# Reordering side work in a two-block transformer kernel: activation sums behind loads, filler between attention stages, sums ahead of taps

## The chip, the cores and the metric

The kernel runs on one core of one Trainium2 chip. The metric is the device time of one execution in microseconds (us). Engines are TensorE (PE, with its weight loads PEld), VectorE (DVE), ScalarE (ACT), GpSimd (POOL) and SyncE (SP, which here issues DMAs).

## The reference

Two transformer blocks run one after the other on a sequence of 1024 tokens of width 1024, all in fp32. The first is a hybrid layer; the second an attention block with a convolutional FFN:

```python
def hybrid_layer(x, ...):
    h = rms_norm(x, norm_g)
    u = jnp.einsum('bsd,dc->bsc', h, w_in)
    v_c, b_c, c_c, z_c, q, k, v, z_a, gate_logits = jnp.split(u, SPLIT_POINTS, axis=-1)
    y_c = b_c * causal_depthwise_conv(c_c * v_c, conv_w) * jax.nn.silu(z_c)
    y_a = jnp.einsum('bsc,cd->bsd', y_c, w_conv_out)
    o = sliding_window_attention(q, k, v, sinks) * jax.nn.silu(z_a)   # q, k normed per head
    y_b = jnp.einsum('bsc,cd->bsd', o, w_attn_out)
    g_a, g_b = jnp.split(jax.nn.sigmoid(gate_logits + gate_b), 2, axis=-1)
    return x + jnp.einsum('bsd,de->bse', g_a * y_a + g_b * y_b, w_out)

def conv_ffn(x, w_up, conv_w, conv_b, w_down):        # FFN_DIM 2816
    u, g = jnp.split(x @ w_up, [FFN_DIM], axis=-1)
    g = causal_dwconv(g, conv_w, conv_b)
    return (jax.nn.gelu(g, approximate=False) * u) @ w_down

def second_block(x, p, ...):
    x = layer_norm(x * ALPHA + fox_mixer(x, ...))     # causal attention with forget gates
    x = layer_norm(x * ALPHA + conv_ffn(x, ...))
    return x + sigmoid(x @ ple_w_gate + ple_b_gate) * (p @ ple_w_proj)
```

The sliding attention has 16 query heads on 4 key heads, blocks of 128 queries and a window of 128.

## The kernel before, in words

Every fp32 product is three matmuls of rounded operands: high by high, high by low, low by high. An operand is split into its halves by a rounding copy on ScalarE (`hi`, L84: names ending in `h`) and a subtraction on VectorE (`lo`, L88 and L90: names ending in `l`). A weight tile is loaded by SyncE into `wraw` (L157) and split into `wh` and `wl`. `gemm_ws` (L173, matmuls L181 to L183) takes eight k tiles, 24 matmuls 128x512, with the weights stationary; `gemm_xs` (L186, L196 and L197) does it with the activations stationary. PSUM has eight banks, each for one 128x512 result.

**Pairs.** Large products are done by a scheme of seven products in place of eight (`seven`, L437). Sums of operand quarters (`X7.build`, L380 for the additions; results `xsh` and `xsl`) are made once; per pair of column tiles the weights' sums are made (`Pairs`, L481 to L553), their halves are `pwh`, `pwl` and `pwo`. A product is 12 matmuls (L433 to L435), in the program's order 1, 2, 6, 5, 7, 3, 4. At product 6 the next pair's weights are loaded, at 7 its first quarter is split (`first`), at 3 its second part is made (`second`), at 4 its third (`third`). Products 1 and 2 read `x2Th` and `x2Tl` in the FFN, the others mostly the sums.

**Attention of the first block** (`attn1_stream`, L631). For 32 items (four groups of heads by eight token tiles) a software pipeline runs stages: `a1` projects, `a2` norms and transposes, `a3` makes scores and exponentials (L696, L704), `a3b` the sums' reciprocal on VectorE (L718) and the normalisation of `p` on GpSimd (L720), `a4` transposes `p` (L731), `a5` multiplies by the values (L745, L746). The loop at L764 calls one stage of five items in turn. `weave` (L32) mixes this stream with the convolution branch and the gates by the cost that each stream yields: the attention goes on while its cost stays under `RATIO` times the other's.

**The FFN.** The last step of the second attention (`attn_out`, L1341) adds, norms (POOL L1370) and stores `x2` per token tile (L1371), and `to_T` (L933) transposes it (L938) into `x2Th` and `x2Tl`. The transposes of the last three tiles are kept in `attn_out.last` and are done in `up_plain` (L1430), which makes the first three column tiles of the inner activation by `gemm_ws`, as `pg0`, `pu0`, `pg1` in the first of them; `ffn_conv` makes the taps (L1404 to L1409) and the gelu. Beside these tiles (L1455 to L1472) the seven products' sums `x7.build` run, a piece at every other step. Then 19 pairs make the other column tiles (L1515). `keep` (L1415) stores the inner activation of two column tiles: three quarters as they are and four sums of quarters (`hs`), made on VectorE, as the operands of the down product: seven stores into `h_d` on SyncE (L1420 to L1429).

The order of each engine's instructions is set by a scheduler, which runs the program on a timeline of its own and hands out tiles from pools (46 of 128x1024 in `t4`, 8 in `y2`).

Of the kernel before, what the change touches and what calls it, by code (L numbers as in the profile page):

```python
# [11 lines left out]
HP = 400  # L12
LAG = 3
NP = 6
RATIO = 1.9
NCONV, NG, NTR = 3, 1, 5
N4, N2 = 46, 8
NPLAIN = 3
# [38 lines left out]
def tile_two_blocks(ctx: ExitStack, tc: tile.TileContext, I, out, dbg=None):  # L57
# [130 lines left out]
    def gemm_xs(x, t, wk, n, ps=None, step=2, kts=range(KT)):  # L188

        if ps is None:  # L190
            ps = bank()
        c = max(107.0, n / 2.4)
        for kt in kts:
            xh, xl = x.sta(kt, t)
            wh, wl = wk(kt)
            pe.matmul(ps[:, :n], lhsT=xh, rhs=wh, start=kt == kts[0], stop=False)  # L196
            pe.matmul(ps[:, :n], lhsT=xh, rhs=wl, start=False, stop=False)  # L197
            pe.matmul(ps[:, :n], lhsT=xl, rhs=wh, start=False, stop=kt == kts[-1])
            if kt % step == step - 1:
                yield 3 * step * c  # L200
        return ps
# [430 lines left out]
    def attn1_stream():  # L632
# [3 lines left out]
        def a1(n):  # L636
            g, t = divmod(n, 8)
            if t == 0:
                grp[g] = dict(W=[wqa.get(0) for _ in range(4)])
                grp[g]["V"] = t4((128, 8, 128), F32R, "V")  # L640
            G = grp[g]
            ps = yield from gemm_xs(hT, t, lambda kt: tuple(p[:, kt % 2, :] for p in G["W"][kt // 2]), 384)
            V = G["V"]
            raw = t2((128, 384), name="qkv")
            act.activation(raw, ps[:, :384], AF.Copy)
            hi(V[:, t, 0:64], ps[:, 320:384])
            sq = t2((128, 320), name="sq")
            dve.tensor_tensor(out=sq, in0=raw[:, :320], in1=raw[:, :320], op=OP.mult)
            ss = sm(5)
            dve.tensor_reduce(out=ss, in_=sq.rearrange("p (h d) -> p h d", d=64), axis=mybir.AxisListType.X,  # L650
                              op=OP.add)
            lo(V[:, t, 64:128], raw[:, 320:384], V[:, t, 0:64])
            r = rstd_of(ss, 5, 1.0 / 64, 1e-6)
            qn = t2((128, 384), name="qn")
            dve.tensor_tensor(out=qn[:, :320].rearrange("p (h d) -> p h d", d=64),
                              in0=raw[:, :320].rearrange("p (h d) -> p h d", d=64),
                              in1=r[:, :, None].to_broadcast([128, 5, 64]), op=OP.mult)
            dve.tensor_scalar(qn[:, 320:384], raw[:, 256:320], r[:, 4:5], None, op0=OP.mult)
            st[n] = dict(qn=qn)
# [104 lines left out]
        for n in range(N + 4):  # L764
            if n < N:
                yield from a1(n)
            if 0 <= n - 2 < N:
                yield from a3(n - 2)
            if 0 <= n - 1 < N:
                yield from a2(n - 1)  # L770
            if 0 <= n - 2 < N:
                a3b(n - 2)
            if 0 <= n - 3 < N:
                yield from a4(n - 3)
            if 0 <= n - 4 < N:
                yield from a5(n - 4)
# [654 lines left out]
    def up_plain(ct, first=False):  # L1431
        wg = wq.get()
        if first:

            pg0 = yield from gemm_ws(wg, x2T, 0)
            wu = wq.get()
            attn_out.last.popleft()()
            attn_out.last.popleft()()
            pu0 = yield from gemm_ws(wu, x2T, 0)
            attn_out.last.popleft()()  # L1440
            pg1 = yield from gemm_ws(wg, x2T, 1)
        gs = t4(name="gs")
        for hf in range(2):
            ps = (pg0, pg1)[hf] if first else (yield from gemm_ws(wg, x2T, hf))
            act.activation(gs[:, HS[hf]], ps, AF.Copy)
        y = ffn_conv(ct, gs)
        if not first:
            wu = wq.get()
        for hf in range(2):
            ps = pu0 if first and hf == 0 else (yield from gemm_ws(wu, x2T, hf))  # L1450
            tt(dve, y[:, HS[hf]], ps, y[:, HS[hf]], OP.mult)
        keep(ct, y)
# [3 lines left out]
    for ct in range(NPLAIN):  # L1456
        for _ in up_plain(ct, first=ct == 0):
            n += 1
            if n == 13:
                build = chain(x7.build(0), x7.build(1))  # L1460
            if n % 2:
                next(build, None)
            if n == 26:
                upairs.load(0)
            elif n == 34:
                upairs.first(0)
            elif n == 40:
                upairs.second(0)
            elif n == 44:
                upairs.third(0)  # L1470
# [28 lines left out]
    def split_down():  # L1499
# [5 lines left out]
            ops2.append((h, l))  # L1505
        raw_down()

    def end_up(i):
        if i == 2:
            for _ in range(4):  # L1510
                raw_down()
        elif i in (3, 4):
            split_down()

    for ct in range(NPLAIN, NCT):  # L1515
        gs, u = upairs.run(end_up if ct == NCT - 1 else None)
        y = ffn_conv(ct, gs)
        tt(dve, y, y, u, OP.mult)
        keep(ct, y)
    split_down()  # L1520

    def residual(t):
# [145 lines left out]
```

## Time and profile before

| what | us |
| --- | --- |
| median of three runs | 2528.01 (2527.15 to 2532.12) |
| profiled execution, its own time | 2526.26 |
| its span | 2524.6 |
| TensorE busy | 2448.2 |
| VectorE busy | 1610.2 |
| ScalarE busy | 1070.2 |
| GpSimd busy | 449.6 |

All times of the trace are counted from the span's start. The mean granted TensorE clock is 0.989 of full speed. The first attention ends at about 424 us, the FFN begins at about 1732, its pairs run from about 1797 to 2215.

### The profile page before, as it was taken

How to read it: one execution, taken by the hardware profiler on the slowest of the kernel's cores; microseconds unless marked ns; L12 is line 12 of the kernel's file. 1: busy time of each engine (PE TensorE's matmuls, PEld its weight loads, DVE VectorE, ACT ScalarE, POOL GpSimd, SP SyncE). 2: the span in 40 equal slices, each digit the busy share in tenths (PEclk: the TensorE clock that was granted, in tenths of full speed). 3: DMA queues.
4: the chain of work that ended last, by engine and by line, in shares of the span. 5: the costliest groups of instructions: out<-in, count | busy, mean ns of one | idle time of the engine just before them, and what ended most of it. 6: DMA issues, size and time to landing. Idle time of an engine off the chain costs nothing. (4 is left out here: it accounts for less than half of the span.)

```text
span 2524.6 us, 33221 instructions
## 1 busy us (share of the span) xinstructions
PE 2448.2 (97%) x12330; PEld 2083.1 (83%) x12330; DVE 1610.2 (64%) x2936; ACT 1070.2 (42%) x1978; POOL 449.6 (18%) x498
## 2 busy tenths in 40 slices
PE   8999998999999999999999999999899999999999
PEld 7988987888888788888989898887677777788887
DVE  4777777666765436325575656567877777676873
ACT  4656566323333312126565656542423232354321
POOL 2322232000000045012323323413000000000331
PEclk9999998999999999999999999999999999999999
DMA  5021111322253889321111122332223232396512
GB/s 166 22 61 53 37 42 51 100 75 67 59 175 109 292 313 369 134 76 52 59 51 59 43 66 85 134 109 92 67 82 102 81 112 81 125 359 229 186 68 84
DMA packets 242924, 285.77 MB, mean 113 GB/s; under 512 B 21826, under 2 KB 166730, under 8 KB 242762
## 3 DMA queue, kind: packets, MB, share of 16 engines
q1 hardware_dynamic: 242762, 283.65, 34.4%
q8 instruction: 97, 1.59, 0.3%
q14 instruction: 65, 0.53, 0.1%
HBM read 206.72 MB, written 76.87 MB: 112 GB/s over the span
## 5 line engine op out<-in xcount | busy, mean ns | idle before, releaser
L433 PE MATMUL ps<-xsh,pwh 128*128 128x512 f32 x456 | 179.2, 393 | 8.0 <-ACT pwh L84 8.0
L434 PE MATMUL ps<-xsl,pwh 128*128 128x512 f32 x456 | 178.4, 391 | 0.0
L88 DVE TENSOR_TENSOR pwl<-wraw,pwh 128x1024 fp32r<-128x1024 f32 x114 | 138.5, 1221 | 60.4 <-ACT pwh L84 60.3
L435 PE MATMUL ps<-xsh,pwl 128*128 128x512 f32 x456 | 171.4, 390 | 0.0
L84 ACT ACTIVATE pwh<-wraw 128x1024 fp32r<-128x1024 f32 x114 | 118.1, 1051 | 112.8 <-DVE wraw L380 104.0
L84 ACT ACTIVATE wh<-wraw 128x1024 fp32r<-128x1024 f32 (+3 forms) x105 | 105.5, 1016 | 73.6 <-DMA wraw<-in_ple_w_gate_dram 18.8
L1337 POOL TENSOR_SCALAR sm<-sm 128x1 f32<-128x1 f32 x16 | 11.6, 724 | 698.0 <-DVE sm L1335 698.0
L1535 PE MATMUL ps<-dh,dl 128*128 128x512 f32 x308 | 119.8, 389 | 0.0
L1534 PE MATMUL ps<-dl,dh 128*128 128x512 f32 x308 | 119.8, 389 | 0.0
L88 DVE TENSOR_TENSOR wl<-wraw,wh 128x1024 fp32r<-128x1024 f32 (+1 forms) x77 | 92.1, 1205 | 43.2 <-ACT wh L84 36.5
L1533 PE MATMUL ps<-dh 128*128 128x512 f32 x308 | 118.1, 390 | 0.0
L88 DVE TENSOR_TENSOR phl<-ps,phl 128x512 fp32r<-128x512 f32 (+1 forms) x160 | 97.3, 633 | 31.9 <-ACT phl L84 30.6
L181 PE MATMUL ps<-hTh,wh 128*128 128x512 f32 x288 | 115.2, 400 | 2.3 <-DVE hTl L90 2.2
L433 PE MATMUL ps<-x2Th,pwh 128*128 128x512 f32 x228 | 93.2, 409 | 22.3 <-ACT pwh L84 22.3
L182 PE MATMUL ps<-hTl,wh 128*128 128x512 f32 x288 | 114.3, 397 | 0.0
L183 PE MATMUL ps<-hTh,wl 128*128 128x512 f32 x288 | 114.3, 397 | 0.0
L84 ACT ACTIVATE dh<-dr 128x1024 fp32r<-128x1024 f32 x77 | 80.2, 1059 | 71.1 <-PE ps L1535 33.4
L433 PEld LDWEIGHTS ps<-xsh,pwh 128*128 128x128 f32 x456 | 86.2, 189 | 28.1 <-ACT pwh L84 10.4
L88 DVE TENSOR_TENSOR dl<-dr,dh 128x1024 fp32r<-128x1024 f32 x77 | 91.9, 1220 | 25.5 <-ACT dh L84 13.9
L380 DVE TENSOR_TENSOR wraw<-wraw 128x512 f32<-128x512 f32 x152 | 105.0, 691 | 4.3
L380 POOL TENSOR_TENSOR wda<-wda 128x512 f32<-128x512 f32 x11 | 15.1, 1377 | 516.7 <-DMA wda<-in_ffn_w_down_dram 495.2
L181 PE MATMUL ps<-x1Th,wh 128*128 128x512 f32 x256 | 101.7, 397 | 1.4 <-DVE QB L90 1.4
(341 smaller groups left out, 7496.1 us busy)
## 6 DMA issues: line engine op xcount, KB each, us to landing
wraw<-in_w_in_dram SPq DMA_DIRECT2D x56, 512.0 KB, 4.4
wraw<-in_ffn_w_up_dram SPq DMA_DIRECT2D x44, 512.0 KB, 6.6
dr<-h_d SPq DMA_DIRECT2D x77, 256.0 KB, 3.5
wraw<-in_attn_w_in_dram SPq DMA_DIRECT2D x22, 512.0 KB, 4.3
h_d<-hs SPq DMA_DIRECT2D x44, 256.0 KB, 2.8
dr<-t_d SPq DMA_DIRECT2D x44, 256.0 KB, 4.3
h_d<-yc SPq DMA_DIRECT2D x33, 256.0 KB, 2.3
dr<-in_ffn_w_down_dram SPq DMA_DIRECT2D x33, 256.0 KB, 5.4
```

The lines of the kernel that those rows point to most:

```text
L84: act.activation(dst, src, AF.Copy, scale=1.0 if scale is None else scale)
L88: (eng or dve).tensor_tensor(out=dst, in0=src, in1=f(h), op=OP.subtract)
L181: pe.matmul(ps, lhsT=w[0][:, kt, :], rhs=xh, start=kt == 0, stop=False)
L182: pe.matmul(ps, lhsT=w[0][:, kt, :], rhs=xl, start=False, stop=False)
L183: pe.matmul(ps, lhsT=w[1][:, kt, :], rhs=xh, start=False, stop=kt == KT - 1)
L380: e.tensor_tensor(out=out, in0=a, in1=b, op=op)
L433: pe.matmul(ps, lhsT=w[0][:, c], rhs=xh, start=st, stop=False, skip_group_check=more)
L434: pe.matmul(ps, lhsT=w[0][:, c], rhs=xl, start=False, stop=False, skip_group_check=more)
L435: pe.matmul(ps, lhsT=w[1][:, c], rhs=xh, start=False, stop=q == 3, skip_group_check=more)
L1533: pe.matmul(ps[j], lhsT=h[:, 0, c], rhs=h[:, 1, :], start=m == 0, stop=False)
L1534: pe.matmul(ps[j], lhsT=h[:, 0, c], rhs=l[:, 1, :], start=False, stop=False)
L1535: pe.matmul(ps[j], lhsT=l[:, 0, c], rhs=h[:, 1, :], start=False, stop=m == NM - 1)
```

## The change

Six edits. (1) `RATIO` goes from 1.9 to 2.1. (2) In `a1`, the next group's first weights are loaded at token tile 6 and split at tile 7, in place of when the group begins. (3) In the four last rounds of the attention's loop, which have no `a1`, the stream yields a cost of 7000 (the other stream's turns are counted in the same unit, ns), so that `weave` gives the other branch a turn there. (4) In the first column tile of the FFN all three kept transposes go behind `pu0`; two of them were ahead. (5) The seven products' sums begin at step 9 in place of 13 and run at every step up to 12, then at every odd one. (6) `keep` of a column tile is done at product 5 of the next pair (behind the load of the pair after, at product 6), in place of right behind its own.

```diff
@@ -12,7 +12,7 @@
 HP = 400
 LAG = 3
 NP = 6
-RATIO = 1.9
+RATIO = 2.1
 NCONV, NG, NTR = 3, 1, 5
 N4, N2 = 46, 8
 NPLAIN = 3
@@ -639,6 +639,10 @@
                 grp[g] = dict(W=[wqa.get(0) for _ in range(4)])
                 grp[g]["V"] = t4((128, 8, 128), F32R, "V")
             G = grp[g]
+            if t == 6:
+                wqa.fetch(2)
+            elif t == 7 and wqa.raw:
+                wqa.split()
             ps = yield from gemm_xs(hT, t, lambda kt: tuple(p[:, kt % 2, :] for p in G["W"][kt // 2]), 384)
             V = G["V"]
             raw = t2((128, 384), name="qkv")
@@ -764,6 +768,8 @@
         for n in range(N + 4):
             if n < N:
                 yield from a1(n)
+            else:
+                yield 7000.0
             if 0 <= n - 2 < N:
                 yield from a3(n - 2)
             if 0 <= n - 1 < N:
@@ -1434,10 +1440,9 @@
 
             pg0 = yield from gemm_ws(wg, x2T, 0)
             wu = wq.get()
-            attn_out.last.popleft()()
-            attn_out.last.popleft()()
             pu0 = yield from gemm_ws(wu, x2T, 0)
-            attn_out.last.popleft()()
+            for _ in range(3):
+                attn_out.last.popleft()()
             pg1 = yield from gemm_ws(wg, x2T, 1)
         gs = t4(name="gs")
         for hf in range(2):
@@ -1456,9 +1461,9 @@
     for ct in range(NPLAIN):
         for _ in up_plain(ct, first=ct == 0):
             n += 1
-            if n == 13:
+            if n == 9:
                 build = chain(x7.build(0), x7.build(1))
-            if n % 2:
+            if n < 13 or n % 2:
                 next(build, None)
             if n == 26:
                 upairs.load(0)
@@ -1505,7 +1510,14 @@
             ops2.append((h, l))
         raw_down()
 
+    kept = deque()
+
+    def beside_up(i):
+        if i == 5 and kept:
+            keep(*kept.popleft())
+
     def end_up(i):
+        beside_up(i)
         if i == 2:
             for _ in range(4):
                 raw_down()
@@ -1513,10 +1525,11 @@
             split_down()
 
     for ct in range(NPLAIN, NCT):
-        gs, u = upairs.run(end_up if ct == NCT - 1 else None)
+        gs, u = upairs.run(end_up if ct == NCT - 1 else beside_up)
         y = ffn_conv(ct, gs)
         tt(dve, y, y, u, OP.mult)
-        keep(ct, y)
+        kept.append((ct, y))
+    keep(*kept.popleft())
     split_down()
 
     def residual(t):
```

Lines of the changed kernel are up to ten higher than those of the kernel before at the same place. Three excerpts of the order follow, each of before and then of the change.

SyncE between an odd column tile's pair and the next pair. `wraw` are a pair's two weight loads, `h0` to `h6` the stores of the inner activation, `yc` its column tiles, `hs` its sums. Before:

```order
L1422 DMA h3_d_284<-yc_17738 128x512
L1429 DMA h4_d_285<-hs_17747 128x512
L1429 DMA h5_d_286<-hs_17748 128x512
L1429 DMA h6_d_287<-hs_17749 128x512
L157 DMA wraw_17794<-in_ffn_w_up_2_dram 128x8x128
L1429 DMA h2_d_283<-hs_17750 128x512
L157 DMA wraw_17796<-in_ffn_w_up_2_dram 128x8x128
L157 DMA wraw_17924<-in_ffn_w_up_2_dram 128x8x128
```

and now:

```order
L157 DMA wraw_17651<-in_ffn_w_up_2_dram 128x8x128
L1426 DMA h0_d_281<-yc_17608 128x512
L157 DMA wraw_17779<-in_ffn_w_up_2_dram 128x8x128
L157 DMA wraw_17781<-in_ffn_w_up_2_dram 128x8x128
L1427 DMA h1_d_282<-yc_17738 128x512
L1428 DMA h3_d_284<-yc_17738 128x512
L1435 DMA h4_d_285<-hs_17800 128x512
L1435 DMA h5_d_286<-hs_17801 128x512
L1435 DMA h6_d_287<-hs_17802 128x512
```

The loads of the next pair stand ahead of all of its stores but `h0`, and the six others ahead of the pair after.

TensorE at the end of the first attention: the last scores (L697, L701), the transposes of `p` (L731, L735), the product with the values (L745 and L746, L749 and L750) and gate projection (L181 to L183). `p1_4637` before and `p1_4589` now are the last item but one, `p1_4686` now the last. Before:

```order
L697 MATMUL ps_4717<-KL_3792,Q_4665 128x256
L697 MATMUL ps_4726<-KL_3792,Q_4665 128x256
L696 MATMUL ps_4726<-KH_3791,Q_4665 128x256
L697 MATMUL ps_4726<-KL_3792,Q_4665 128x256
L731 MATMUL ps_4745<-ident_71,p1_4637 128x128
L731 MATMUL ps_4754<-ident_71,p1_4637 128x128
L745 MATMUL ps_4763<-ph_4684,V_3589 128x512
L746 MATMUL ps_4763<-pl_4685,V_3589 128x512
L745 MATMUL ps_4763<-ph_4693,V_3589 128x512
```

and now, from the last but one's value product to the last item's transposes:

```order
L750 MATMUL ps_4735<-pl_4643,V_3541 128x512
L749 MATMUL ps_4735<-ph_4651,V_3541 128x512
L750 MATMUL ps_4735<-pl_4652,V_3541 128x512
L182 MATMUL ps_4667<-hTl_419,wh_4150 128x512
L183 MATMUL ps_4667<-hTh_418,wl_4151 128x512
L181 MATMUL ps_4760<-hTh_184,wh_4563 128x512
...
L181 MATMUL ps_4760<-hTh_232,wh_4563 128x512
L182 MATMUL ps_4760<-hTl_233,wh_4563 128x512
L183 MATMUL ps_4760<-hTh_232,wl_4564 128x512
L735 MATMUL ps_4773<-ident_71,p1_4686 128x128
L735 MATMUL ps_4782<-ident_71,p1_4686 128x128
```

Before, the transposes come directly behind scores; now 26 projection matmuls (20 of them in the gap) stand ahead of those of the last item.

ScalarE at the start of the FFN: the evictions of the transposes (`x2Th`, L84) and the split of the next weights (`wh_16856`). Before, the end of the second kept set, the weights, and the third:

```order
L84 ACTIVATE x2Th_16806<-ps_16892 128x2x128
L84 ACTIVATE x2Th_16813<-ps_16897 128x2x128
L84 ACTIVATE wh_16856<-wraw_16827 128x1024
L1445 ACTIVATE gs_16972<-ps_16831 128x512
L84 ACTIVATE x2Th_16792<-ps_16927 128x2x128
```

and now:

```order
L84 ACTIVATE x2Th_16806<-ps_16803 128x2x128
L84 ACTIVATE x2Th_16813<-ps_16810 128x2x128
L84 ACTIVATE wh_16856<-wraw_16827 128x1024
L84 ACTIVATE x2Th_16792<-ps_16887 128x2x128
L84 ACTIVATE x2Th_16799<-ps_16892 128x2x128
L84 ACTIVATE x2Th_16806<-ps_16897 128x2x128
```

The weights' split stands ahead of all three kept sets' evictions, where it stood ahead of one.

## Rows read from the trace of the kernel before

**Rows 1.** The page's first part: busy us of each engine, share of the span, x instructions.

```profile
PE 2448.2 (97%) x12330; PEld 2083.1 (83%) x12330; DVE 1610.2 (64%) x2936; ACT 1070.2 (42%) x1978; POOL 449.6 (18%) x498
```

**Rows 2.** The list of TensorE's waits over the span: line of the waiting matmul, releaser, us in total, times, longest us.

```profile
PE ps L433 <- ACT pwh L84: 30.3, 10, 8.0
PE ps L731 <- POOL p L720: 8.4, 7, 3.6
...
PE ps L938 <- POOL xn L1370: 2.4, 1, 2.4
```

**Rows 3.** The page's grouped lines, the one of the products that read x2Th: busy us, mean ns of one, idle us before them and what ended most of it.

```profile
L433 PE MATMUL ps<-x2Th,pwh 128*128 128x512 f32 x228 | 93.2, 409 | 22.3 <-ACT pwh L84 22.3
```

**Rows 4.** Windows of 100 us, a full stretch first: length, busy us and (x instructions) of PE, PEld, DVE, ACT and POOL, the granted clock, DMA share, GB/s.

```profile
500.00:600.00 100.00, 100.00 (x440) 82.16 (x439) 66.36 (x80) 33.34 (x40) 0.00 (x0) 1.00 0.23 69
1800.00:1900.00 100.00, 87.69 (x364) 70.47 (x363) 69.60 (x83) 32.22 (x38) 0.00 (x0) 0.93 0.29 85
1900.00:2000.00 100.00, 94.35 (x397) 77.07 (x396) 71.89 (x85) 34.09 (x40) 0.00 (x0) 0.95 0.29 87
2000.00:2100.00 100.00, 95.45 (x418) 77.72 (x417) 73.44 (x89) 32.15 (x37) 0.00 (x0) 1.00 0.27 82
2100.00:2200.00 100.00, 91.47 (x391) 73.66 (x390) 69.27 (x85) 32.04 (x38) 0.00 (x0) 0.98 0.40 124
```

**Rows 5.** Windows of 10 us behind long waits of TensorE, the same columns.

```profile
410.00:420.00 10.00, 6.29 (x20) 4.17 (x18) 9.96 (x17) 7.04 (x16) 4.69 (x6) 0.67 0.00 0
420.00:430.00 10.00, 8.13 (x27) 6.05 (x28) 4.91 (x7) 2.79 (x5) 2.03 (x2) 0.67 0.00 0
1740.00:1750.00 10.00, 7.45 (x28) 5.84 (x29) 6.45 (x14) 2.87 (x6) 4.30 (x4) 0.83 0.83 237
1820.00:1830.00 10.00, 9.33 (x30) 7.29 (x31) 4.19 (x4) 3.74 (x5) 0.00 (x0) 0.69 0.38 105
1850.00:1860.00 10.00, 7.82 (x28) 5.68 (x27) 5.68 (x9) 2.28 (x3) 0.00 (x0) 0.84 1.02 283
1940.00:1950.00 10.00, 9.86 (x32) 7.91 (x33) 7.55 (x9) 4.55 (x7) 0.00 (x0) 0.72 0.43 109
1980.00:1990.00 10.00, 7.83 (x28) 6.04 (x27) 6.67 (x9) 3.96 (x6) 0.00 (x0) 0.83 0.80 220
2110.00:2120.00 10.00, 10.00 (x39) 8.12 (x40) 8.43 (x11) 5.07 (x6) 0.00 (x0) 0.86 0.17 43
```

**Rows 6.** The timeline of SyncE's DMA issues between two pairs; columns: start in us from the span's start, us, engine, line, operation, out<-in, shape, count, and in brackets the idle time before it and what ended it.

```profile
1848.15 1.33 SPq L1429 DMA_DIRECT2D h_d<-hs  x3
1849.57 0.44 SPq L157 DMA_DIRECT2D wraw<-in_ffn_w_up_dram  x1
...
1851.04 4.06 SPq L157 DMA_DIRECT2D wraw<-in_ffn_w_up_dram  x3
```

**Rows 7.** The timeline of VectorE at the same place, same columns.

```profile
1845.66 1.23 DVE L380 TENSOR_TENSOR yc<-yc,pb 128x1024 f32<-128x1024 f32 x1 [1.19 <-ACT yc L1409]
1846.92 0.69 DVE L380 TENSOR_TENSOR hs<-yc 128x512 f32<-128x512 f32 x1
```

**Rows 8.** The timeline of ScalarE at the same place, same columns.

```profile
1854.47 1.06 ACT L84 ACTIVATE pwh<-wraw 128x1024 fp32r<-128x1024 f32 x1 [0.38 <-DMA wraw<-in_ffn_w_up_dram]
```

**Rows 9.** The timeline of TensorE at the same place: the last matmul of one pair and the first of the next.

```profile
1853.07 0.39 PE L435 MATMUL ps<-xsh,pwl 128*128 128x512 f32 x1
1855.58 0.50 PE L433 MATMUL ps<-x2Th,pwh 128*128 128x512 f32 x1 [2.12 <-ACT pwh L84]
```

**Rows 10.** The timeline of TensorE at the end of the first attention, the transposes (L731) behind a wait.

```profile
409.62 0.69 PE L731 MATMUL ps<-ident,p 128*128 128x128 f32 x2 [2.37 <-POOL p L720]
...
416.78 0.69 PE L731 MATMUL ps<-ident,p 128*128 128x128 f32 x2 [3.57 <-POOL p L720]
```

**Rows 11.** The timeline of ScalarE there: table load, gate, the last item's exponentials (one of four shown).

```profile
407.81 1.28 ACT L794 ACT_TABLE_LOAD   x1
409.10 0.69 ACT L794 ACTIVATE gt<-ps,pv 128x512 f32<-128x512 f32 x1
...
411.10 0.51 ACT L704 ACTIVATE p<-p,sm 128x256 f32<-128x256 f32 x1
```

**Rows 12.** The timeline of TensorE at the first matmuls of a later group of the attention's projection.

```profile
226.18 0.44 PE L196 MATMUL ps<-wh,hTh 128*128 128x384 f32 x1 [0.46 <-ACT wh L84]
227.17 0.44 PE L197 MATMUL ps<-wl,hTh 128*128 128x384 f32 x1 [0.55 <-DVE wl L88]
```

**Rows 13.** The timeline of SyncE's issues at the start of the FFN.

```profile
1741.60 2.97 SPq L157 DMA_DIRECT2D wraw<-in_ffn_w_up_dram  x3
```

**Rows 14.** The timeline of ScalarE at the start of the FFN.

```profile
1747.34 1.06 ACT L84 ACTIVATE wh<-wraw 128x1024 fp32r<-128x1024 f32 x1 [3.05 <-DMA wraw<-in_ffn_w_up_dram]
```

**Rows 15.** The timeline of VectorE at the start of the FFN.

```profile
1748.43 1.23 DVE L88 TENSOR_TENSOR wl<-wraw,wh 128x1024 fp32r<-128x1024 f32 x1 [1.61 <-ACT wh L84]
1751.78 1.42 DVE L88 TENSOR_TENSOR x2Tl<-ps,x2Th 128x256 fp32r<-128x256 f32 x4 [2.12 <-ACT x2Th L84]
...
1763.80 1.28 DVE L1405 SCALAR_TENSOR_TENSOR yc<-gs,pv,yc 128x1023 f32<-128x1023 f32 x1 [8.34 <-ACT yc L1404]
```

**Rows 16.** The timeline of GpSimd at the end of the first attention, the normalisation of two items.

```profile
409.08 1.85 POOL L720 TENSOR_SCALAR p<-p,sm 128x256 f32<-128x256 f32 x4 [5.40 <-DVE sm L718]
416.24 5.79 POOL L720 TENSOR_SCALAR p<-p,sm 128x256 f32<-128x256 f32 x4 [5.31 <-ACT xsh L84]
```


## Prediction

> **What bounds the kernel now.** I read the engines' busy times first [rows 1]: TensorE is busy 97% of the span, so matmuls set the time, and both kernels issue the same 12330. A change of order can win only TensorE's idle time, about 76 us of the 2524.6, and what its clock loses after idle stretches. The list of TensorE's waits names the places [rows 2]: 30.3 us for `pwh` from ScalarE, 8.4 us for the attention's normalised `p` from GpSimd, 2.4 us for `xn` from GpSimd. The grouped lines split the first [rows 3]: 22.3 us stand ahead of products that read `x2Th` (the first of a pair), and its longest wait, 8.0 us, is a single one ahead of the first product on a sum `xsh`. Then the windows. A full stretch holds 440 matmuls in 100 us at clock 1.00 [rows 4], one each 0.227 us, so a product of 12 is 2.73 us and a pair of seven is 19.1 us. The four stretches from 1800 to 2200 hold 364 + 397 + 418 + 391 = 1570: 190 are missing, 43 us, of which 31.0 are idle (400 less the busy 368.96) and about 12 are clock. The 10-us rows show the clock at 0.67 to 0.86 right behind the waits [rows 5], the mean of full speed (2.4 GHz) and stretches at half of it (1.2 GHz); (1 - clock) x 10 us is about what a row lost. This is what the change can give back.
>
> **Pairs of the inner activation (edit 6).** Before, SyncE issues the three sums' stores (L1429) at 1848.15, the next pair's first load at 1849.57 behind them, and the rest at 1851.04 behind one more sum's store [rows 6]. Those stores wait for VectorE: `y` times `u` at 1845.66, then four sums of 0.69 [rows 7]. So a load whose buffer had long been free starts when the sums are done. ScalarE rounds it at 1854.47 [rows 8]; TensorE, whose last product's last matmul began at 1853.07, goes on at 1855.58 [rows 9]. Nine such places make the 22.3 us. After the change SyncE has the pair's loads ahead of the sums' stores, and the next pair's behind them. What is then queued behind the waiting stores is only the pair after, and by the order its load is issued about 22 us ahead of need, which is more than the 5 us from issue at 1849.57 to ScalarE's use at 1854.47. What is late next is VectorE: it now does the sums inside the next pair. I lay its instructions end to end in the new order, with 1.23 for 128x1024 and 0.69 for 128x512 [rows 7]: the low half that product 6 of a pair needs ends some 25.8 us after the pair before began. By the order that product stands fourth (behind two of its own pair and the last of the pair before), so its use comes at 19.1 + 3 x 2.73 = 27.3: 1.5 us to spare, the least of the margins I find. All VectorE work of two pairs is about 29 of 38 us. So I take the whole wait as gone: 22.3 idle, and the clock of 1850, 1940, 1980 and 2110, 1.6 + 2.8 + 1.7 + 1.4 = 7.5 [rows 5]. **29.8 us**. Below: if each of nine margins is missed by 1.5 us (all that this least one has to spare, again), 13.5 less, 16. Above: nothing more is there, 32.
>
> **The first attention's end (edits 1 to 3).** TensorE waits at 409.62 (2.37) and 416.78 (3.57) for GpSimd's `p` [rows 10], all such waits are 8.4 [rows 2], and the rows 410 and 420 lost 3.3 each to the clock [rows 5], about 1 of it while idle: 8.4 + 5.6 = 14.0 in all. The filler puts projection matmuls between the last scores and the transposes that need `p`: by the order, 26 ahead of the last item's first transposes (second excerpt of the order) and the item's own four, against four and no filler before. For the last two items I count about 8 us of TensorE work each between scores and transposes, against 2.7 and 1.8. What the items need: before, the last one's scores end at about 407.2 and its transposes start at 416.78, 9.5 us. On ScalarE that stretch holds two table loads of 1.28 around one gate eviction of 0.69, and four exponentials of 0.51 [rows 11]. After, the last item has a second gate eviction, a third table load and a weight split among the same exponentials: 9.5 + 0.69 + 1.28 = 11.5, less what the order saves on VectorE ahead of the reciprocal, 11.0 to 11.7. So the last but one is covered (6.6 of 8.0) and the last still waits 3.3 to 3.7; one low clock stretch of 1.7 to 3.4 follows. 14.0 - 3.7 - 2.6 = **7.7 us**. Nothing is queued for the moved work's own sake: the projection only runs earlier, so 6 us less of it stand between attention and the first sum products, whose sums VectorE ends 2 us ahead of use now: I allow -1. Edit 2 fetches a group's first weights two tiles early: the waits 0.46 and 0.55 for `wh` and `wl` [rows 12] go, **+1**. Edit 1 shares the work out elsewhere, with no sign I can read: 0, bounds -3 and +3. The three edits: **7.7**, bounds 0 and 14.
>
> Here the trace speaks against a rule. The table load of 407.81 takes 1.28 and the gate eviction starts at 409.10, 0.01 us behind it [rows 11]. The Trainium skill ("ScalarE: Activation LUTs", What ACT_TABLE_LOAD costs) puts a drain of about 1.38 us behind each load, 2.66 us a switch. By that the third load would cost the last item 1.4 us more and the three edits would give 6.3; by the row they give 7.7, and I go by the row.
>
> **The FFN's front (edits 4 and 5).** Edit 4 moves three sets of transposes from both sides of `pu0` to behind it. Before: 2.36 + 1.34 idle (the second one behind 1743.26) and 1.7 of clock [rows 5], 5.4. After, the order of ScalarE has the split of the next weights (`wh_16856`) ahead of all twelve evictions of these transposes. That load is issued at 1741.60 [rows 13] and ScalarE starts on it at 1747.34, after 3.05 of waiting for it [rows 14]; VectorE's `wl` runs 1748.43 to 1749.66 [rows 15]. TensorE ends `pu0` at about 1743.3, fills the free PSUM banks with transposes and then waits: the low halves follow `wl` at 1.42/4 = 0.355 each [rows 15], eleven of twelve until `pg1` can start, some 1753. With 3 us of transposes in between it idles about 6.4 and then loses 1.7 to 3.4 of clock: 8.9, so edit 4 **loses 3.5** (bounds: 8 lost, 4 won if the load lands as soon as the queue is free). Edit 5: VectorE idles 8.34 us at 1763.80 behind a tap that waits [rows 15], and later the first sum product waits 8.0 for `pwh` [rows 2], plus 2.7 of clock (half speed from 1820.67 to about 1826 [rows 5]). With sums started from step 9 and built in every step, those sums stand ahead of the waiting tap; VectorE reaches the low half of that product at about 1814.6 where TensorE needs it at 1815. I take 10 of 10.75 as won (bounds 6 and 10.75). Edits 4 and 5 together: **6.5**, bounds 0 and 14.
>
> **Sum.** 29.8 + 7.7 + 6.5 = 44.0 us. The profiled execution took 2526.26 (1.7 outside its span), 1.75 below the median: 2482.3 by its own time, 2484.0 on the median's level. I forecast **2484**.
>
> **Rivals.**
> *New waits take half.* VectorE's margin of 1.5 us in a pair was laid out by hand, and the loads now run beside seven stores. If nine pairs wait 1.5 us each, 13.5 go, 2497.5; if attention's end and the front's sums give nothing either, another 14, 2511. For it: VectorE at 70 to 73% in these stretches [rows 4]. Against: even pairs, loaded early, show no wait today.
> *Attention's end gives nothing.* GpSimd's four normalisations took 1.85 us at 409.08 but 5.79 at 416.24 [rows 16], while VectorE ran additions and low halves of 1.2 us on two operands; the new order again has sums right behind the reciprocal. If both last items meet this, each chain is up to 3.9 longer and the 7.7 are lost: 2491.7. The Trainium skill has a rule for it ("SBUF — State Buffer", Who interferes with whom): a VectorE operation with two inputs in SBUF blocks a GpSimd operation that reads SBUF for its whole length. The rows agree with it. Against the rival: the first quarter alone decides the first wait, and filler now stands between the later ones.
> *Slower.* The loads stay late while VectorE and ScalarE have taken on more ahead of the pair's start. If a pair's first load is still issued some 4 us ahead of use, as at 1849.57, then `y` times `u` and four sums (1.23 + 4 x 0.69 = 4.0) stand ahead of the pair's low halves, and nine pairs lose that again plus the waits that stay: 9 x 3.3 = 30 on top of before, less 14 elsewhere: 2544. It decides as soon as the first load waits for a store behind it; the order shows the loads ahead, so it would take a buffer freed late.
> *More.* The last attention wait and the front's new wait are covered too: 6.3 + 8.9 more, 2469.
>
> **Chances.** Forecast 0.50; new waits 0.18; attention gives nothing 0.14; more 0.14; slower 0.04. Range 2467 to 2503: it takes in the forecast, *more*, *attention* and the nearer part of *new waits*. 0.2% of this time is 5 us, about what a measurement can tell: faster 0.94, same 0.02, slower 0.04.
>
> **What would show it.** Right: loads of `wraw` ahead of the sums' stores on SyncE and no waits of `x2Th` products for `pwh`; windows of 1850 to 2200 near 440 matmuls per 100 us; one wait of 3 to 4 us for `p` at the attention's end; a new wait of about 6 us behind `pu0` on `x2Th` or `x2Tl`; no 8 us ahead of the first sum product. Wrong: waits of 1 to 3 us inside pairs on VectorE's `pwl`, or a front whose sums are late again.

## The result

The changed kernel takes 2469.24 us (median of four runs, 2467.99 to 2471.10) beside 2527.58 of the kernel before (2521.45 to 2532.12): a ratio of 0.977, interval 0.975 to 0.979. The forecast was 2484.0 in 2467 to 2503. The profiled execution's span is 2466.3 us, 58.3 less than before, at a mean clock of 0.997 instead of 0.989. The first part of the page and rows of the list of TensorE's waits (line, releaser, us in total, times, longest), the answers to [rows 1, 2]:

```profile
PE 2422.6 (98%) x12330; PEld 2073.3 (84%) x12330; DVE 1609.8 (65%) x2936; ACT 1066.6 (43%) x1976; POOL 451.8 (18%) x498
```

```profile
...
PE ps L735 <- POOL p L724: 7.1, 2, 4.9
PE ps L944 <- DVE x2Tl L88: 4.3, 1, 4.3
PE ps L181 <- ACT wh L84: 4.2, 2, 2.9
...
PE ps L433 <- DVE pb L380: 0.8, 1, 0.8
```

The 30.3 us for `pwh` are gone from the list. The waits for GpSimd's `p` are two in place of seven, and the longest has grown from 3.6 to 4.9. A new one of 4.3 stands at the FFN's front. Three windows in the pairs, the answer to [rows 4] (length, busy us and counts of PE, PEld, DVE, ACT, POOL, clock, DMA share, GB/s):

```profile
1800.00:1900.00 100.00, 100.00 (x443) 82.78 (x442) 74.63 (x90) 34.77 (x42) 0.00 (x0) 1.00 0.34 100
1900.00:2000.00 100.00, 100.00 (x443) 82.81 (x442) 79.50 (x96) 34.92 (x42) 0.00 (x0) 1.00 0.36 111
2000.00:2100.00 100.00, 100.00 (x443) 82.81 (x442) 80.54 (x98) 34.33 (x41) 0.00 (x0) 1.00 0.36 109
```

TensorE is busy throughout at clock 1.00, with 443 matmuls in 100 us where 364 to 418 stood before. VectorE, which now does the sums inside the pairs, rises to 75 to 81%.

To give each microsecond its place, I took for every matmul the time to the start of the next, less the median of that for matmuls of the same line and operands: the loss over the matmuls' own spacing, in which waits and half clock (1.2 GHz) are one sum. By stretch of the program:

| stretch | before | after | edits 1-3 | edit 6 alone | edit 4 undone |
| --- | --- | --- | --- | --- | --- |
| first 50 us | 6.9 | 5.9 | 6.9 | 5.8 | 7.0 |
| 50 to 240 us | 5.7 | 0.0 | 0.2 | 6.0 | -0.2 |
| 240 to the attention's end | 2.1 | 2.1 | 2.0 | 2.3 | 1.9 |
| the attention's end (some 42 us) | 14.8 | 7.3 | 6.1 | 14.7 | 7.2 |
| on to the FFN | 11.6 | 11.8 | 11.7 | 9.3 | 13.8 |
| the FFN's front | 6.1 | 6.8 | 6.7 | 5.6 | 6.7 |
| its first column tiles | 0.3 | 1.4 | 0.3 | 0.3 | 2.4 |
| first sum products | 11.2 | 0.3 | 11.4 | 10.8 | 0.3 |
| pairs | 35.5 | 0.6 | 37.1 | 0.7 | 0.6 |

The columns on the right are of experiments below. From before to after this sums to 58 us: 34.9 from the pairs, 10.9 from the first sum products, 7.5 from the attention's end, 5.7 from its first half, 1.0 at the very start, less 1.8 at the FFN's front and its first column tiles. The 1.0 at the start isn't the change's: no edit touches that place, and before ran at a granted clock of 0.72 from 16 to 22 us where after ran at 1.00, as edit 6 alone did too. The pairs' row moves by chance as well: four kernels below that leave the pairs as they were (edits 1 to 3; edit 2; edits 1 and 3; edit 1) lost 33.4 to 41.3 there, as stretches at half clock came or stayed away, so the 34.9 is good to some us.

### The profile page after: what moved, and what is told of

It is laid out like the page before. It is cut to its first block, busy times and chain, and to the rows that moved or that the text cites. A ratio compares the mean times of both kernels' runs of the same rounds, so it can differ in the third digit from the quotient of the medians.

```text
span 2466.3 us, 33200 instructions
## 1 busy us (share of the span) xinstructions
PE 2422.6 (98%) x12330; PEld 2073.3 (84%) x12330; DVE 1609.8 (65%) x2936; ACT 1066.6 (43%) x1976; POOL 451.8 (18%) x498
## 4 chain that ended last, share of the span: by engine, by line
PE 90%; DVE 4%; ACT 2%; issue 1%; DMA 1%; POOL 1%; SPq 0%; ACTq 0%; POOLq 0%; DVEq 0%
PE ps L433 10%; PE ps L435 10%; PE ps L434 10%; PE ps L181 7%; PE ps L182 7%; PE ps L183 7%; PE ps L196 5%; PE ps L197 5%; PE ps L198 5%; PE ps L1547 3%; PE ps L1546 3%; PE ps L1548 3%; PE ps L1129 2%; PE ps L1153 1%; PE ps L1152 1%; PE ps L1096 1%
## 5 line engine op out<-in xcount | busy, mean ns | idle before, releaser
L84 ACT ACTIVATE wh<-wraw 128x1024 fp32r<-128x1024 f32 (+3 forms) x105 | 105.7, 1017 | 67.0 <-DMA wraw<-in_attn_w_out_dram 15.5
L1343 POOL TENSOR_SCALAR sm<-sm 128x1 f32<-128x1 f32 x16 | 11.6, 725 | 654.8 <-DVE sm L1341 654.8
L84 ACT ACTIVATE pwh<-wraw 128x1024 fp32r<-128x1024 f32 x114 | 118.2, 1051 | 27.0 <-DVE wraw L380 23.7
L449 ACT ACTIVATE u<-ps 128x512 f32<-128x512 f32 x38 | 22.7, 598 | 236.7 <-PE ps L435 236.7
L181 PE MATMUL ps<-hTh,wh 128*128 128x512 f32 x288 | 114.1, 397 | 2.9 <-DVE hTl L90 2.7
L183 PE MATMUL ps<-hTh,wl 128*128 128x512 f32 x288 | 113.9, 396 | 0.0
L84 ACT ACTIVATE dh<-dr 128x1024 fp32r<-128x1024 f32 x77 | 80.0, 1058 | 71.4 <-PE ps L1548 35.3
L380 POOL TENSOR_TENSOR wda<-wda 128x512 f32<-128x512 f32 x11 | 14.8, 1348 | 516.0 <-DMA wda<-in_ffn_w_down_dram 499.9
L181 PE MATMUL ps<-x1Th,wh 128*128 128x512 f32 x256 | 101.6, 397 | 1.4 <-DVE QB L90 1.4
```

The source lines that it names most:

```text
L84: act.activation(dst, src, AF.Copy, scale=1.0 if scale is None else scale)
L181: pe.matmul(ps, lhsT=w[0][:, kt, :], rhs=xh, start=kt == 0, stop=False)
L183: pe.matmul(ps, lhsT=w[1][:, kt, :], rhs=xh, start=False, stop=kt == KT - 1)
```

## The experiments

Each is compared with runs of the kernel before on the same chip; the medians of before moved between 2524.8 and 2529.4 from one group to the next, so ratios are given, and small differences are read from the loss by stretch, which is that of one profiled execution.

**Edit 6 alone.** The edit is the last hunks of the change's diff (`kept`, `beside_up`).

> Only edit 6 (stores and sums of the inner activation behind the next loads). Theory A, the loads stood behind stores that wait for VectorE's sums on SyncE: all nine waits ahead of the first products of a pair go, 35 us less (22.3 of waits, the rest half clock and the first matmuls behind a wait), 2493. Rival B, the edits need each other (the sums of the seven products have to be early for the pairs to keep pace): under 25 us less, above 2503, with waits inside the pairs.

Measured: 2488.90 beside 2529.38, ratio 0.984 (0.983 to 0.986). The list of TensorE's waits of this run:

```profile
PE ps L731 <- POOL p L720: 8.4, 7, 3.6
PE ps L433 <- ACT pwh L84: 8.0, 1, 8.0
```

Of ten waits for `pwh` one is left, that of the first sum product; the loss in the pairs is 0.7. Theory A holds, rival B falls: the pairs keep pace without the early sums. Of the 40 us by the medians, 35 are the pairs'; the rest lies in stretches that the edit doesn't touch (3.4 of it on the way to the FFN and in the first 50 us).

**The stores issued by GpSimd.**

```diff
-        sp.dma_start(out=h_d[0][m], in_=a[:, HS[0]])
+        pool.dma_start(out=h_d[0][m], in_=a[:, HS[0]])
...
-            sp.dma_start(out=h_d[i][m], in_=x)
+            pool.dma_start(out=h_d[i][m], in_=x)
```

> The kernel before with the inner activation's seven stores of a pair issued by GpSimd instead of SyncE; the sums stay where they were on VectorE. Theory A (queue order on SyncE): the loads no longer stand behind anything, the nine waits go, about 35 us less, 2493. Rival C (VectorE's four sums at the pair's end delay the next pair's splits): the waits stay, 2528, within 5.

Measured: 2496.83, ratio 0.987 (0.985 to 0.989). VectorE's timeline and GpSimd's between an odd pair and the next (start, us, engine, line, operation, operands, shape, count, idle before):

```profile
1842.84 1.22 DVE L380 TENSOR_TENSOR yc<-yc,pb 128x1024 f32<-128x1024 f32 x1 [1.19 <-ACT yc L1409]
1844.10 0.69 DVE L380 TENSOR_TENSOR hs<-yc 128x512 f32<-128x512 f32 x1
1844.83 0.69 DVE L380 TENSOR_TENSOR hs<-hs,yc 128x512 f32<-128x512 f32 x1
1845.43 0.69 DVE L380 TENSOR_TENSOR hs<-yc 128x512 f32<-128x512 f32 x1
1846.04 0.69 DVE L380 TENSOR_TENSOR hs<-yc,hs 128x512 f32<-128x512 f32 x1
1846.64 0.69 DVE L380 TENSOR_TENSOR pa<-ps,u 128x512 f32<-128x512 f32 x1
1847.24 1.22 DVE L88 TENSOR_TENSOR pwl<-wraw,pwh 128x1024 fp32r<-128x1024 f32 x1
```

```profile
1845.42 2.22 POOL L1429 DMA_DIRECT2D h_d<-hs  x4
```

The sums stand on VectorE where they stood, ahead of the next pair's low half (1847.24), as in [rows 7]; the stores wait for them on GpSimd and hold up nobody. TensorE's list names one wait for `pwh`, 8.0 us, and none ahead of the first products of a pair. So the wait was SyncE's order, not VectorE's work: rival C falls for these waits. The pairs lose 3.8 here where edit 6 leaves 0.7, and this rest is VectorE's: in nine pairs product 6 is held 0.3 by a low half that is late (it ends at 1859.25, and the matmul that reads it starts at 1859.30).

**The sums made by GpSimd.**

```diff
-        tt(dve, s1, a[:, HS[1]], b[:, HS[1]], OP.add)
+        tt(pool, s1, a[:, HS[1]], b[:, HS[1]], OP.add)
...
-        tt(dve, s4, b[:, HS[0]], s2, OP.subtract)
+        tt(pool, s4, b[:, HS[0]], s2, OP.subtract)
```

> The kernel before with the four sums made by GpSimd instead of VectorE, stores still on SyncE, the first load behind two of the sums' stores. Theory A: the first load still waits for y times u and two sums, now about 1.4 us each on GpSimd, and is issued about as late as before: within 8 us of 2528, waits ahead of the pairs as before. Rival C (VectorE's sums are what costs): VectorE is 2.6 us freer at nine places, 15 to 25 us less, 2503 to 2513.

Measured: 2542.05, ratio 1.005 (1.003 to 1.007), slower. SyncE's issues, GpSimd's sums, the split that waits for the load, and two windows in the pairs:

```profile
1852.79 1.69 SPq L1429 DMA_DIRECT2D h_d<-hs  x2
1854.58 1.11 SPq L157 DMA_DIRECT2D wraw<-in_ffn_w_up_dram  x2
```

```profile
1851.47 1.29 POOL L380 TENSOR_TENSOR hs<-yc 128x512 f32<-128x512 f32 x1 [50.92 <-DVE yc L380]
1852.84 1.29 POOL L380 TENSOR_TENSOR hs<-hs,yc 128x512 f32<-128x512 f32 x1
```

```profile
1858.91 1.06 ACT L84 ACTIVATE pwh<-wraw 128x1024 fp32r<-128x1024 f32 x1 [8.29 <-DMA wraw<-in_ffn_w_up_dram]
```

```profile
1900.00:2000.00 100.00, 89.98 (x363) 72.82 (x364) 62.67 (x74) 32.31 (x39) 10.13 (x8) 0.91 0.34 103
2000.00:2100.00 100.00, 94.13 (x396) 76.90 (x395) 63.96 (x74) 31.56 (x38) 10.13 (x8) 0.95 0.26 82
```

The load is issued at 1854.58, behind the stores of two sums that end at 1854.1; ScalarE waits 8.29 us, and TensorE's waits for `pwh` rise from 30.3 to 33.5. VectorE's share fell to 63 and 64% of the windows from 1900 to 2100 (72 to 73% before [rows 4]), and the kernel got slower: the sign that theory A asks for and rival C excludes. Its size, 13 us (12 of it in the pairs, which lose 47.8), is above the 8 that I allowed: the load goes out 3.4 us ahead of the odd pair's end (1857.96), before it was 3.9 (1849.57 and 1853.46), and both waits and half-clock stretches behind them grew. The waits for `pwh` account for 3.2 of the 12; most of the rest is the clock (0.91 and 0.95 in the two windows, 0.95 and 1.00 before), and why it fell so much oftener no run here shows.

**Edits 1 to 3 alone.**

> Only edits 1 to 3 (the attention's share, its weights two tiles early, the filler). By the trace after: 13.7 us less, 2514, of which the attention's end (398 to 440 us) 7.4 and the stretch before 240 us 5.6. Rival: the edits meet elsewhere and the part before 240 us is chance in the clock (a half-clock stretch that one profile shows and another not): 8 us less, 2520.

Measured: 2514.95, ratio 0.994 (0.992 to 0.996). The loss falls by 5.5 between 50 and 240 us and by 8.7 at the end, much as in the full change (5.7 and 7.5). So it isn't chance in the clock.

**Edit 2 alone.**

> Only edit 2 (a group's first weights fetched and split two tiles early). In the trace after, the stretch from 50 to 240 us lost 5.6 us less over its matmuls' own time than before, with the waits for wh and wl at 226 us gone. Theory: edit 2 made it: 3 to 5 us less of loss between 50 and 240 us, 2523 to 2525, the attention's end as before (14.8 lost from 398 to 440). Rival: the share of 2.1 made it, and edit 2 alone takes away the 1.0 us of those two waits and no more.

Measured: 2518.75 beside 2527.61, ratio 0.997 (0.995 to 0.998). The loss from 50 to 240 us falls from 5.7 to -0.6; that at the attention's end stays, 16.0. Edit 2 made the first-half gain (the whole profile loses 6.0 less), and more than its two waits [rows 12]: the waits for `V` at 140 and 229 us and a half-clock stretch (228.7 to 232.1) that followed them go as well.

**Edits 1 and 3, and edit 1 alone.** Edit 3 by itself was tried too and gave no result: the program asks that over 32 steps of the other branch be left behind the attention, beside which the first block's sums are built, and at 1.9 the filler leaves fewer. What had been expected of it, 2520 with 7 or 8 lost at the attention's end, stays open.

> Edits 1 and 3 (the share of 2.1 and the filler), without edit 2. Theory: they make the attention's end and edit 2 makes the stretch before 240 us: the loss from 50 to 240 us stays at 5 to 6 as before, that at the attention's end falls from 14.8 to 6 to 8; 2519 to 2521. Rival: the filler needs edit 2 as well (the other branch's work comes in another order): the end loses more than 10.

> Edit 1 alone (the attention's share 2.1 instead of 1.9). Theory: it moves work of the other branch behind the attention, which only the filler brings back into its end: no gain of its own, the end loses 14 to 18, 2527 to 2531. Rival: the share itself fills the end: the loss there falls below 10.

Measured: edits 1 and 3, 2529.53 beside 2526.18, ratio 1.001 (1.000 to 1.003); edit 1, 2532.63, ratio 1.002 (1.001 to 1.003). The waits in the two lists:

```profile
PE ps L731 <- POOL p L720: 7.5, 4, 4.9
...
PE ps L696 <- DVE Q L90: 3.2, 1, 3.2
```

```profile
PE ps L731 <- POOL p L720: 12.6, 5, 9.7
...
PE ps L696 <- DVE Q L90: 3.7, 2, 3.2
```

With edit 1 alone one wait for `p` is 9.7 us and the end loses 15.5; with the filler it is 4.9 and the end loses 6.2. That much I expected. What I had not: with the share at 2.1 and the late weights, the group change at 330 us waits 3.2 for `Q`, the stretch from 240 us to the end loses 7.5 in place of 2.1, and that from 50 to 240 us, expected at 5 to 6, loses 7.7 (8.0 with edit 1 alone). Up to the attention's end edits 1 and 3 lose 28.2 in place of 29.5: of the filler's 8.6 only 1.3 is left. (Their pairs lost 41.3 in this profile, 5.8 more than before, with nothing changed there; the median holds such chance too.) With edit 2 the two stretches are at 0.2 and 2.0. So of the 14 us of the three edits none is one edit's own but edit 2's 6: the filler is of use once the early weights are there, and by the program it needs the share.

**Edit 4 undone.**

> The changed kernel with edit 4 undone (two of the kept sets of transposes ahead of pu0 again). By the traces edit 4 cost: the stretch from the FFN's start to the first sums lost 6.1 us over its matmuls' own time before and 8.2 after, so 2 us less than the change, 2467, with waits of 2.4 and 1.3 for xn and x2Tl in place of the one of 4.3. Rival: the early sums (edit 5) need the transposes together, and the first sum product waits again: 3 us or more above the change.

Measured: 2470.67, ratio 0.978 (0.976 to 0.980), the change's own 0.977. The front loses 6.7 + 2.4 without edit 4 and 6.8 + 1.4 with it. Neither the theory nor the rival holds: the edit cost nothing here, and gained at most 1 us.

**The last normalisation on VectorE.**

```diff
-                pool.tensor_scalar(p[:, hh, o:], p[:, hh, o:], den[:, hh:hh + 1], 1.0, op0=OP.mult, op1=OP.mult)
+                (dve if n > 30 else pool).tensor_scalar(p[:, hh, o:], p[:, hh, o:], den[:, hh:hh + 1], 1.0, ...)
```

> The changed kernel with the last item's normalisation of p on VectorE instead of GpSimd. Theory L: on GpSimd the first two quarters took 2.35 and 2.49 us beside VectorE's additions of two operands, against 0.48 where VectorE does none, and TensorE waited for the first of them; on VectorE they follow the reciprocal at once, and the 4.9 us wait falls by about 1.8 to 3.0; 2 to 4 us less in all. Rival S: ScalarE's work ahead of the reciprocal alone sets the wait: it falls by under 0.5.

Measured: 2465.39, ratio 0.976 (0.975 to 0.978). TensorE's wait falls from 4.86 to 2.73, the loss at the attention's end from 7.3 to 3.9. In the change GpSimd starts at 403.50, and these are VectorE's rows beside it, then GpSimd's and TensorE's:

```profile
402.27 0.42 DVE L759 TENSOR_TENSOR O<-ps,tmp 64x256 f32<-64x256 f32 x1 [0.63 <-ACT tmp L758]
402.70 0.43 DVE L760 TENSOR_TENSOR O<-ps,tmp 64x256 f32<-64x256 f32 x1
403.16 0.18 DVE L722 RECIPROCAL sm<-sm 128x4 f32<-128x4 f32 x1
403.26 1.19 DVE L380 TENSOR_TENSOR xs<-hTl 128x1024 f32<-128x1024 f32 x1
404.37 1.22 DVE L380 TENSOR_TENSOR xt<-hTh 128x1024 f32<-128x1024 f32 x1
```

```profile
403.50 5.74 POOL L724 TENSOR_SCALAR p<-p,sm 128x256 f32<-128x256 f32 x4 [12.24 <-issue]
```

```profile
405.90 0.69 PE L735 MATMUL ps<-ident,p 128*128 128x128 f32 x2 [4.86 <-POOL p L724]
```

The four quarters took 2.35, 2.49, 0.48 and 0.48: the first is held beside the two additions, and the transposes start when it is done. In the experiment the four take 1.14 us on VectorE at 404.05. Theory L holds for 2.1 us of the wait; 2.7 are left, so it isn't all.

**The small exponentials early.**

```diff
+                    if n > 30:
+                        act.activation(e[:, hh:hh + 1], nsink[:, 4 * g + hh:4 * g + hh + 1], AF.Exp,
+                                       bias=mn[:, hh:hh + 1], scale=-1.0)
...
+            if n <= 30:
-            dve.tensor_tensor(out=e, in0=mn, in1=nsink[:, 4 * g:4 * g + 4], op=OP.subtract)
-            act.activation(e, e, AF.Exp)
+                dve.tensor_tensor(out=e, in0=mn, in1=nsink[:, 4 * g:4 * g + 4], op=OP.subtract)
+                act.activation(e, e, AF.Exp)
```

> The changed kernel with the last item's small exponentials (of minimum less sink) taken per head right behind its large ones, so that no table load and gate eviction stand between. Theory S: in the change 4.0 us of two table loads, a gate eviction and a rounding stand between the last large exponential (ends 397.4) and the small one's end (401.4), all on the chain to the reciprocal; the wait of 4.9 falls by 3 to 4, 4 to 7 us less in all with its clock stretch. Rival L: GpSimd's quarters beside VectorE's additions set the wait, which falls by less than 2.

Measured: 2463.13, ratio 0.975 (0.973 to 0.976). ScalarE in the change, from the last large exponential's read to the small one, and GpSimd in the experiment:

```profile
397.25 0.19 ACT L708 ACTIVATION_READ_ACCUMULATOR p<-p,sm 128x1 f32 x1
397.46 1.28 ACT L800 ACT_TABLE_LOAD   x1
398.75 0.69 ACT L800 ACTIVATE gt<-ps,pv 128x512 f32<-128x512 f32 x1
399.34 0.59 ACT L84 ACTIVATE ph<-ps 128x512 fp32r<-128x512 f32 x1
399.95 1.28 ACT L714 ACT_TABLE_LOAD   x1
401.24 0.21 ACT L714 ACTIVATE sm<-sm 128x4 f32<-128x4 f32 x1
```

```profile
400.91 1.84 POOL L728 TENSOR_SCALAR p<-p,sm 128x256 f32<-128x256 f32 x4 [7.51 <-ACT sm L712]
```

In the change the small exponential of 0.21 us stands behind a gate, a rounding and two table loads, 4 us. Taken at once, GpSimd starts at 400.91 in place of 403.50, and ahead of VectorE's additions, so that its four quarters take 1.84; TensorE's wait for the last item is gone and the end loses nothing; the ratio is 0.002 under the change's, some 5 us. Theory S holds, and with it goes the wait that theory L explains. One thing more moved along: in the change VectorE makes two additions for the item before (402.27 and 402.70, with 0.63 of waiting for ScalarE) ahead of the reciprocal, 1.5 us of the chain, and here the reciprocal goes first (400.58). The experiment doesn't part this from the table loads.

**The stores of x2 by GpSimd.**

```diff
-                sp.dma_start(out=x2_d[t * 128:(t + 1) * 128, :], in_=xn)
+                pool.dma_start(out=x2_d[t * 128:(t + 1) * 128, :], in_=xn)
```

> The changed kernel with the stores of x2 issued by GpSimd, which makes it, instead of SyncE. Theory Q: SyncE stands 5.6 us behind two of these stores (1721.76) and so issues the weights' load late, and ScalarE's split of these weights stands ahead of the transposes' evictions; with the load early the wait of 4.3 falls to about 2.2, which GpSimd's last xn (ready at 1732.6) sets: 2 to 4 us less. Rival: issuing costs GpSimd time in the chain to xn, the wait stays or grows: 0 to 5 us more.

Measured: 2467.44, ratio 0.977 (0.975 to 0.978); the interval doesn't part it from the change, the trace does. The front loses 3.2 in place of 6.8, its waits are 1.4 and 1.1 in place of 4.3; the first column tiles lose 2.5 in place of 1.4. Theory Q holds for the wait; the net is about 2.4 us.

**Both together.**

> The changed kernel with both of what helped by the traces: the last item's small exponentials right behind its large ones, and the stores of x2 issued by GpSimd. If the gains are of separate places they add: 7.9 us less of loss at the attention's end and 2.4 at the FFN's front, 2459, a ratio of 0.973 to the kernel before. If one is chance in the clock: 2462 or more.

Measured: 2459.31 (2458.52 to 2460.94), ratio 0.973 (0.971 to 0.975). This beats the change; the two gains add.

## Why the prediction was right, and where it was short

**Pairs.** The mechanism is the one forecast: two loads ahead of the six stores. SyncE's issues after, beside [rows 6]:

```profile
1845.39 3.97 SPq L157 DMA_DIRECT2D wraw<-in_ffn_w_up_dram  x2
1864.04 0.34 SPq L1427 DMA_DIRECT2D h_d<-yc  x1
1864.43 0.42 SPq L1428 DMA_DIRECT2D h_d<-yc  x1
1864.95 2.19 SPq L1435 DMA_DIRECT2D h_d<-hs  x4
1867.18 1.57 SPq L157 DMA_DIRECT2D wraw<-in_ffn_w_up_dram  x2
```

The loads that go out at 1845.39 are for the pair that TensorE begins at 1868.03. The stores (L1427 to L1435) follow 19 us later, still in the pair ahead of it, and the loads behind them at 1867.18 are for the pair after. ScalarE's first rounding of the one and the other:

```profile
1860.57 1.05 ACT L84 ACTIVATE pwh<-wraw 128x1024 fp32r<-128x1024 f32 x1
...
1879.61 1.05 ACT L84 ACTIVATE pwh<-wraw 128x1024 fp32r<-128x1024 f32 x1
```

So the later load goes out 12.4 us ahead of its use, not the 22 that the prediction counted, and that is still more than the 5 that a load took. No wait inside a pair appeared: the low half for product 6 ends at 1855.75 and is first read at 1857.61, 1.9 to spare where 1.5 was forecast, and rival *new waits* fell with it. The term was too small: 29.8 forecast, 34.9 measured. What was mis-sized is the price of a wait: the prediction took the page's idle time (22.3) and the clock rows (7.5) as the whole. Before, from 1840 to 2215 us, ten starts behind a wait are 24.7 us late by the spacing of starts (the idle time counts from a matmul's end, 0.39 us after its start, where the next could start after 0.227), the half-clock stretches lost 7.5, and the first matmuls behind a wait, spaced 0.34 to 0.68 at full clock, another 3.4: 35.5 in all, the table's number. The windows had it: at 443 a full stretch, 202 matmuls are missing from 1800 to 2200, 45.6 us, and the pairs and the first sum products gave 45.8 together.

**Attention's end.** 7.7 forecast, 7.5 measured, by errors that cancel; that the number fits is luck. I expected a wait of 3.3 to 3.7 (a chain of 11.0 to 11.7 less 8 gives 3.0 to 3.7); it is 4.86. TensorE's work from the last scores to the wait was 7.7 us, about the 8 counted, but the chain took 12.6. The third table load came as said (loads at 393.58, 397.46 and 399.95 behind the scores' end at 393.3). What I set aside is the rival's mechanism, on the ground that "the first quarter alone decides": the first quarter itself was held 1.87 us (2.35 less 0.48) beside VectorE's additions. The Trainium skill ("SBUF — State Buffer", Who interferes with whom) says that a VectorE operation with two SBUF inputs blocks a GpSimd operation that reads SBUF; the rows agree, 2.35 beside such additions against 0.48 without. Against that the end had lost 14.8 before and not 14.0, and the clock took 2.4 and not 2.6.

The table load's rule goes as the prediction judged: the loads at 397.46 and 399.95 take 1.28 and the next operation starts 0.01 behind. The Trainium skill's drain of 1.38 us behind each ("ScalarE: Activation LUTs", What ACT_TABLE_LOAD costs) has no room in these rows.

**Edit 2.** Forecast +1, measured 5.5 to 6.3. I priced the two waits of one group change and not the stretch: the `V` waits at both group changes and the half clock behind them came from the same late start. The -1 allowed for the first sum products was right to 0.6 (that stretch lost 0.3 before and 0.9 after).

**FFN's front.** Forecast: edit 4 loses 3.5, with `wh` ahead of the evictions. The wait came where it was said, for the reason that was said:

```profile
1721.76 5.60 SPq L1377 DMA_DIRECT2D x_d<-xn  x2
1727.45 2.84 SPq L157 DMA_DIRECT2D wraw<-in_ffn_w_up_dram  x3
```

```profile
1732.11 1.06 ACT L84 ACTIVATE wh<-wraw 128x1024 fp32r<-128x1024 f32 x1 [13.22 <-DMA wraw<-in_ffn_w_up_dram]
1733.08 1.74 ACT L84 ACTIVATE x2Th<-ps 128x256 fp32r<-128x256 f32 x6
```

```profile
1734.34 4.17 DVE L88 TENSOR_TENSOR x2Tl<-ps,x2Th 128x256 fp32r<-128x256 f32 x12
```

```profile
1734.82 2.82 PE L944 MATMUL ps<-ident,xn 128*128 128x128 f32 x12 [4.30 <-DVE x2Tl L88]
```

SyncE stands 5.6 us behind two stores of `x2`, issues the load at 1727.45, and ScalarE, idle 13.22, splits it before it evicts a transpose. The size was off: TensorE goes on as soon as the first low half frees a bank, not when eleven of twelve are done, so the wait is 4.3 and not 6.4 (from 1743.3 to 1753 less 3 is 6.7 by the prediction's own numbers), and the front loses 0.7 more than before, not 3.5. With edit 4 undone it loses as much (6.7), so even the 0.7 isn't shown to be edit 4's. The other 1.1 comes with edit 5 and was not forecast: at 1782.26 ScalarE splits a weight behind the rounding of an early sum (`xsh`, 1781.29, idle 5.42 for VectorE), and TensorE waits 1.24. The first sum products lose 10.9 less where 10 were forecast, and the 8 us wait is gone. Edit 5 was not run by itself; without it the stretch loses 11.4 and 10.8 (edits 1 to 3, edit 6 alone) and with it 0.3, edit 4 undone or not, which leaves it as the cause.

**Sum.** The terms were 29.8, 7.7 and 6.5, measured 34.9, 13.0 and 9.1; with the 1.0 of the start 58 us came of the 44 forecast. The two that were most short were short the same way: the idle time of the named waits was priced, and what follows a wait, or the waits that share its cause, was not. The rival *more* gave 2469 for another reason, a covered attention and front; both waits are there, so the number is no proof of it.

## What to carry to other kernels

A load that waits behind a store on one queue waits for whatever the store's data wait for; look at what stands ahead of a late load on its queue before blaming the engine that is named as the releaser. Price a recurring wait by the matmuls missing from a window against a full one, not by its idle time, which leaves out the restart. An edit that is worth nothing alone (the share, or the share with the filler) can pay once another is there, so undo edits one at a time and also try them alone.

## What the runs showed of the hardware

GpSimd's quarter of 128x256 takes 0.48 us alone and 2.35 to 2.50 beside VectorE's additions and low halves of 128x1024 with two operands. GpSimd issued the inner activation's stores (0.54 us each) and held up nothing, since it had no other work in the pairs. Behind a wait, matmuls are spaced 0.34 to 0.68 us for a few starts even at full clock, against 0.227.
